# A one-core transformer kernel: the first stage's norm, columns and operand splits rearranged over the engines

## The chip, the cores and the metric

The kernel runs on one core of one Trainium2 chip. The metric is device time in microseconds (us), from the start of the program to its end; the time before is the median of three runs. In the profile, PE is TensorE's matmul, PEld its weight load, DVE is VectorE, ACT is ScalarE, POOL is GpSimd and SP is the SyncE queue, from which every load is issued.

## What is computed

The reference is two model blocks in a row on 512 positions of width 1024, all in float32. Only the start of the first block matters here:

```python
mod = cond @ ada_w[layer] + ada_b[layer]          # cond = silu(c)
sh1, sc1, g1, sh2, sc2, g2 = jnp.split(mod, 6, axis=-1)
h = _modulate(_rmsnorm(x, norm1_g[layer]), sh1, sc1)   # h*(1+scale)+shift
y = _pool_mixer(h, pool_w_in, pool_w_grp, pool_scale, pool_w_out)
x = x + g1 * y
h = _modulate(_rmsnorm(x, norm2_g[layer]), sh2, sc2)
x = x + g2 * _conv_ffn(h, ...)
```

Layer 0 uses the pooling mixer, layer 1 a dilated attention with keys and values of their own modulated norm; both have the gated FFN with a short convolution. The second block (retention, stick-breaking attention, FFN) follows.

## The kernel before

**Layout.** x is held as eight tiles x[m] of 128 channels by 512 positions. Weights come as 434 units of 512 KB (eight 128x128 tiles), in the order of their use.

**Exact products from three.** An operand t is split into a high part h (rounded on ACT) and a low part l = t - h; `mm3` (L243) multiplies high by high, high by low and low by high, so one float32 product is three matmuls (L244, L245, L246). A weight unit is split in `issue` (L176): ACT makes `wh` (L182), and `wl` (L184) is made by GpSimd for odd units while `st["spread"]` is set, else by VectorE. Activations are split by `split` (L310) and `modulate` (L479).

**The adaptive columns.** Each of 14 vectors (8 columns each) is a row-by-row dot product of a loaded 512 KB tile with `cond`, on VectorE. `ada_first` (L342) makes the scale and shift of the first norm from half tiles (L362, L364); `ada_chunk` (L329) makes the other 12, one column a step (L336), from tiles that share six `raw` buffers with the weight units.

**Order.** Tile schedules each engine's queue from a simulated list schedule, so the order on an engine need not be that of the text. PE's planner clock `pe["clk"]` adds 0.65 for a product; `pump` (L229) after each product lets side streams emit their next step once the clock is past their due time. Stream 2 is `ada_all` (L370): from clock 38.0, a step every `rate` (2.0 in the first stage, 6.0 afterwards). `need` (L379) forces missing steps at once.

**First stage**, `pool_mixer` (L526). Squares of x (ACT L400) are summed (`Stat`, L402), their mean taken by four one-column products on PE (L251), the root by Ln, Exp and four small VectorE instructions (L428 to L436), and spread to a 128x512 tile by four more products. x times that root is made by GpSimd for seven tiles (L544) and VectorE for one (L546). For each of eight input tiles: its columns (L362, L364, L566), `modulate` (VectorE L483, ACT L488, then the low part on VectorE or GpSimd, L489), then 24 matmuls into eight accumulators of PSUM (`us`). The second half of the last two tiles' products is put off to the end (`late`). Then come the evictions, the pooling bands (L593), the grouped product (`pool_w_grp`) and the output product (`pool_w_out`), whose results are added to x in `done` (L611, L612), which also feeds the next norm (L402) and splits x for it (L319).

**Norms further on.** A layer's next stage starts before its norm is known: `gemm_raw` (L288) multiplies raw x by the first four weight columns and corrects them later (`unraw`, L519: L521 and L522). Meanwhile `norm_gen` (L493), in stream 1, yields 2.5, takes the mean and root, yields 2.5, spreads it, multiplies all x (L473 or L475), and modulates. `conv_ffn` (L627) does so for both layers, `attention` (L900) for two modulated norms of one x (16 tiles).

Of the kernel before, what the change touches and what calls it, by code (L numbers as in the profile page):

```python
# [126 lines left out]
def model_kernel(ctx, tc, xT, wstream, adaw, vecs, crow, tab, rope, dret, selt, bandt, outT, plan, stop=None):  # L127
    nc = tc.nc
# [3 lines left out]
    sp = ctx.enter_context(tc.tile_pool(name="sp", bufs=60))  # L132
# [24 lines left out]
    for m in range(KT):  # L157
        nc.sync.dma_start(x[m], xT[m])
# [6 lines left out]
    nc.sync.dma_start(vec, vecs)  # L165
    nc.sync.dma_start(ct[:, :384], tab[:, :384])
# [7 lines left out]
    st = {"issued": 0, "used": 0, "spread": True}  # L174

    def issue():  # L176
        u = st["issued"]
        st["issued"] += 1
        raw = wp.tile([P, 8, P], F32, tag="raw", name=nm("raw"), bufs=6)
        nc.sync.dma_start(raw, wstream[u])  # L180
        h = wp.tile([P, 8, P], F32R, tag="wh", name=nm("wh"))
        nc.scalar.activation(h, raw, AF.Copy)  # L182
        l = wp.tile([P, 8, P], F32R, tag="wl", name=nm("wl"))
        (nc.gpsimd if u % 2 and st["spread"] else nc.vector).tensor_tensor(l, raw, h.bitcast(F32), op=ALU.subtract)  # L184
        units[u] = (h, l, raw)

    def wt(name, idx, k0, m0, n=1):
        i = st["used"]
        u, j = divmod(i, 8)
        if j == 0:  # L190
            while st["issued"] < min(u + 3, N_UNITS):
                issue()
            units.pop(u - 1, None)
# [135 lines left out]
    def ada_chunk(key):  # L329
# [12 lines left out]
    def ada_first(key):  # L342

        m = cp.tile([P, KT], F32, name=nm("mod"))
        mods[key] = m
        tiles = {}

        def load(j):
            for i in range(2):
                t = tiles[j, i] = S()  # L350
                nc.sync.dma_start(t, adaw[ADA_POS[key], j, :, i * T:i * T + T])

        load(0)
        yield
        for j in range(KT):
            col = small(2, "adaf")
            if j + 1 < KT:
                load(j + 1)
            for i in range(2):
                t = tiles.pop((j, i))  # L360
                half = slice(i * T, i * T + T)
                nc.vector.scalar_tensor_tensor(t, t, 1.0, cond[:, half], op0=ALU.mult, op1=ALU.mult,  # L362
                                               accum_out=col[:, i:i + 1])
            nc.vector.scalar_tensor_tensor(m[:, j:j + 1], col[:, 0:1], col[:, 1:2], ada_bias(key)[:, j:j + 1],  # L364
                                           op0=ALU.add, op1=ALU.add)
            yield
# [99 lines left out]

    def normed(R, residues):
        out = []
        for m in range(KT):
            t = S()  # L470
            if residues:
                to, r = (a.rearrange("p (r i) -> p r i", r=4) for a in (t, R))
                nc.vector.tensor_tensor(to, perm(x[m], 4), r, op=ALU.mult)  # L473
            else:
                nc.vector.tensor_tensor(t, x[m], R, op=ALU.mult)  # L475
            out.append(t)
        return out

    def modulate(xn, gs, sh, marks=None):  # L479
        hs = []  # L480
        for m in range(len(xn)):
            t = S()
            ts = nc.vector.tensor_scalar(t, xn[m], gs[:, m:m + 1], sh[:, m:m + 1], op0=ALU.mult, op1=ALU.add)  # L483
            if marks is not None:
                marks.append(ts.ins)
            h = S(F32R)
            l = S(F32R)
            nc.scalar.activation(h, t, AF.Copy)  # L488
            (nc.gpsimd if m % 2 else nc.vector).tensor_tensor(l, t, h.bitcast(F32), op=ALU.subtract)  # L489
            hs.append((h, l))  # L490
        return hs

    def norm_gen(stat, specs, out, residues):  # L493
        yield 2.5
# [3 lines left out]
        xn = normed(out["R"], residues)  # L498
        out["h"] = [modulate(xn, gs, sh) for gs, sh in specs]

    class RawNorm:


        def __init__(self, gs):
            self.stat, self.gs, self.raw = Stat(), gs, []
# [20 lines left out]
    def pool_mixer(g1, nx):  # L526

        stat = Stat(KT)
        for m in range(KT):
            stat.add(m)  # L530
        lnexp()
        scale_col, shift_col = ada_first((0, 1)), ada_first((0, 0))
        next(scale_col)
        next(shift_col)
        issue()
        next(scale_col)
        next(shift_col)
        Rp = spread(rstd(stat.mean()))
        R = S()
        nc.scalar.activation(R, Rp, AF.Copy)  # L540
        xn = [S() for _ in range(KT)]
        for m in range(KT):
            if m:
                nc.gpsimd.tensor_tensor(xn[m], x[m], R, op=ALU.mult)  # L544
            else:
                nc.vector.tensor_tensor(xn[m], x[m], Rp, op=ALU.mult)  # L546
# [4 lines left out]
        us = [[ps() for _ in range(NB)] for _ in range(2)]  # L551
        gs = cp.tile([P, KT], F32, name="gs0")
        h = []

        def half(i, kt, wH, wL):
            for b in range(NB):
                xH, xL = (a[:, b * P:(b + 1) * P] for a in h[kt])
                mm3(us[i][b], xH, xL, wH, wL, kt == 0, kt == KT - 1)

        late, marks = [], []  # L560
        for m in range(KT):
            if m:
                with tc.issue_after(marks[m - 1]):
                    next(scale_col)
                    next(shift_col)
            nc.vector.scalar_tensor_tensor(gs[:, m:m + 1], mods[(0, 1)][:, m:m + 1], 1.0, V("norm1_g", m),  # L566
                                           op0=ALU.add, op1=ALU.mult)
            h += modulate(xn[m:m + 1], gs[:, m:m + 1], mods[(0, 0)][:, m:m + 1], marks)
            for i in range(2):
                w = wt("pool_w_in", (0,), m * P, i * T, n=4)  # L570
                if i and m >= KT - 2:
                    late.append((m, w))
                else:
                    half(i, m, *w)
        for m, w in late:
            half(1, m, *w)
        ut = [[None] * NB for _ in range(2)]
        for i in range(2):
            for b in range(NB):
                t = ut[i][b] = S()  # L580
                if b % 2:
                    nc.scalar.activation(t, us[i][b], AF.Copy)
                else:
                    nc.vector.tensor_copy(t, us[i][b])
        nc.sync.dma_start(ct[:, 384:], tab[:, 384:])
        pooled = []
        for m in range(KT):
# [7 lines left out]
            pooled.append(split(o))  # L595
        ys = []
# [4 lines left out]
        g1 = g1()  # L601
        nx = nx()
# [14 lines left out]
        part(pss, ms, kts)  # L617
        for o, m in zip(pss, ms):
# [8 lines left out]
    def conv_ffn(l, nx, sh, gsh, g2, after):  # L627
# [3 lines left out]
        for half in range(2):  # L631
# [13 lines left out]
            it = gemms(outs, h)  # L645
# [531 lines left out]
    def next_norm(name, l, key):  # L1177
        def f():
            need(key)
            return RawNorm(gain(V(name, 8 * l, 8), mods[key]))  # L1180
        return f

    rate[0] = 2.0
    nx = pool_mixer(mod((0, 2)), next_norm("norm2_g", 0, (0, 4)))
# [208 lines left out]
```

## Time and profile before

| | us |
|---|---|
| median of 3 runs (lowest, highest) | 2739.53 (2738.41, 2740.74) |
| the profiled execution's own time | 2741.72 |
| its span, first to last instruction | 2740.0 |
| busy: PE / DVE / ACT / POOL | 2651.2 / 1435.7 / 993.5 / 391.4 |

The profile has one core, so the slowest core is the only one. A view of stretches gives the busy time of each engine between two times of the span, with the mean granted TensorE clock as a share of its full level. A view of waits lists for how long an engine sat idle and which instruction ended it. A timeline lists instructions in order, with the idle time just before one in brackets.

### The profile page before, as it was taken

The page shows a single profiled execution, that of the slowest core. Times are in us where ns is not written, and L with a number is a line of the kernel's source. Part 1 is how long each engine was busy: PE and PEld are TensorE (multiplying, and loading weights), DVE is VectorE, ACT ScalarE, POOL GpSimd, SP SyncE. Part 2 cuts the span into 40 slices and gives each one's busy share as a digit, 9 for nine tenths or more (in the row PEclk, how much of TensorE's full clock was granted, in tenths as well). Part 3 has the DMA queues.
Part 4 walks back from the last instruction along what each step waited for, and adds up shares of the span by engine and source line. Part 5 has one row for each costly group of instructions (what it writes and reads, how often), then busy time and mean ns, then how long its engine had stood idle before and what let it go on. Part 6 is the DMA issues. An engine that isn't in the chain of part 4 may idle for free. (4 is left out here: it accounts for less than half of the span.)

```text
span 2740.0 us, 32562 instructions
## 1 busy us (share of the span) xinstructions
PE 2651.2 (97%) x12952; PEld 2186.7 (80%) x12952; DVE 1435.7 (52%) x2146; ACT 993.5 (36%) x1673; POOL 391.4 (14%) x280
## 2 busy tenths in 40 slices
PE   6979999989999999999999999999999999999998
PEld 4868888868788887788888887888888887888887
DVE  8997566782434335853444347543344347543342
ACT  3334233344343443442344451422233451422223
POOL 3220000131212121300003111110111011110111
PEclk9989999999999999999999999999999999999999
DMA  8755555432222222232323211322323211232221
GB/s 293 254 182 189 176 173 173 140 126 75 70 78 73 74 70 78 75 99 97 100 92 116 85 64 52 100 94 98 100 93 118 89 63 54 93 100 94 99 99 47
DMA packets 86231, 297.69 MB, mean 109 GB/s; under 512 B 9574, under 2 KB 10302, under 8 KB 86078
## 3 DMA queue, kind: packets, MB, share of 16 engines
q1 hardware_dynamic: 86078, 295.61, 32.6%
q8 instruction: 101, 1.65, 0.2%
q14 instruction: 52, 0.43, 0.0%
HBM read 293.48 MB, written 2.10 MB: 108 GB/s over the span
## 5 line engine op out<-in xcount | busy, mean ns | idle before, releaser
L244 PE MATMUL ps<-s,wh 128*128 128x512 f32 x3152 | 1244.9, 395 | 0.8 <-DVE s L917 0.6
L245 PE MATMUL ps<-s,wh 128*128 128x512 f32 x3152 | 1235.4, 392 | 6.3 <-POOL s L489 5.6
L246 PE MATMUL ps<-s,wl 128*128 128x512 f32 x3152 | 1232.9, 391 | 3.5 <-DVE wl L184 3.5
L182 ACT ACTIVATE wh<-raw 128x1024 fp32r<-128x1024 f32 x434 | 459.6, 1059 | 1037.6 <-PE ps L245 738.3
L184 DVE TENSOR_TENSOR wl<-raw,wh 128x1024 fp32r<-128x1024 f32 x384 | 481.8, 1255 | 481.1 <-ACT wh L182 468.6
L244 PEld LDWEIGHTS ps<-s,wh 128*128 128x128 f32 x3152 | 594.8, 189 | 132.3 <-issue 8.0
L245 PEld LDWEIGHTS ps<-s,wh 128*128 128x128 f32 x3152 | 595.4, 189 | 128.3 <-POOL s L489 8.5
L246 PEld LDWEIGHTS ps<-s,wl 128*128 128x128 f32 x3152 | 594.5, 189 | 129.3 <-DVE wl L184 3.9
L184 POOL TENSOR_TENSOR wl<-raw,wh 128x1024 fp32r<-128x1024 f32 x50 | 125.4, 2508 | 467.7 <-ACT wh L182 447.9
L402 POOL TENSOR_TENSOR s<-s,s 128x512 f32<-128x512 f32 x45 | 71.6, 1596 | 780.4 <-ACT s L400 727.2
L251 PE MATMUL ps<-s,s 128*64 128x128 f32 (+7 forms) x1376 | 153.6, 305 | 16.2 <-POOL s L1116 12.3
L251 PEld LDWEIGHTS ps<-s,s 128*128 128x128 f32 (+2 forms) x1376 | 122.3, 172 | 53.7 <-issue 17.6
L1149 POOL TENSOR_TENSOR s<-s,s 128x512 f32<-128x512 f32 x44 | 76.2, 1732 | 536.8 <-ACT s L421 536.8
L336 DVE SCALAR_TENSOR_TENSOR araw<-araw,cond 128x1024 f32<-128x1024 f32 x96 | 130.8, 1367 | 36.5 <-DMA araw<-in_adaw 34.6
L1151 DVE TENSOR_TENSOR s<-s,ps 128x512 f32<-128x512 f32 x44 | 30.3, 688 | 140.3 <-PE ps L246 127.8
L421 ACT ACTIVATE s<-s 128x512 f32<-128x512 f32 x96 | 59.7, 625 | 110.1 <-DVE s L653 86.4
L780 ACT ACTIVATE s<-s,st 128x128 f32<-128x128 f32 (+1 forms) x192 | 79.6, 417 | 41.5 <-DVE st L776 27.0
L315 ACT ACTIVATE s<-s 128x512 fp32r<-128x512 f32 x104 | 65.6, 631 | 61.8 <-POOL s L895 41.3
L316 DVE TENSOR_TENSOR s<-s,s 128x512 fp32r<-128x512 f32 x104 | 72.8, 700 | 25.7 <-ACT s L315 25.7
L1146 DVE TENSOR_TENSOR s<-ps,s 128x512 f32<-128x512 f32 x44 | 30.4, 691 | 106.4 <-PE ps L246 106.4
L244 PE MATMUL ps<-wh,s 128*128 128x512 f32 x192 | 77.7, 405 | 7.9 <-ACT s L488 7.9
L246 PE MATMUL ps<-wh,s 128*128 128x512 f32 x192 | 75.9, 397 | 6.1 <-DVE s L489 6.1
(182 smaller groups left out, 2077.8 us busy)
## 6 DMA issues: line engine op xcount, KB each, us to landing
raw<-in_wstream SPq DMA_DIRECT2D x434, 512.0 KB, 3.3
araw<-in_adaw SPq DMA_DIRECT2D x96, 512.0 KB, 4.0
s<-in_adaw SPq DMA_DIRECT2D x32, 256.0 KB, 6.0
x<-in_xT SPq DMA_DIRECT2D x8, 256.0 KB, 5.7
s<-in_dret SPq DMA_DIRECT2D x8, 256.0 KB, 4.8
out<-s SPq DMA_DIRECT2D x8, 256.0 KB, 2.9
s<-in_rope SPq DMA_DIRECT2D x4, 256.0 KB, 5.8
cond<-in_crow SPq DMA_DIRECT2D x1, 512.0 KB, 4.2
```

Source lines behind the costliest of these rows:

```text
L182: nc.scalar.activation(h, raw, AF.Copy)
L184: (nc.gpsimd if u % 2 and st["spread"] else nc.vector).tensor_tensor(l, raw, h.bitcast(F32), op=ALU.subtract)
L244: nc.tensor.matmul(out, wH, xH, start=start, stop=False, **kw)
L245: nc.tensor.matmul(out, wH, xL, start=False, stop=False, **kw)
L246: nc.tensor.matmul(out, wL, xH, start=False, stop=stop, **kw)
L251: nc.tensor.matmul(out, lhsT, rhs, start=start, stop=stop, **kw)
L315: nc.scalar.activation(h, src, AF.Copy)
L316: nc.vector.tensor_tensor(l, src, h.bitcast(F32), op=ALU.subtract)
L336: nc.vector.scalar_tensor_tensor(raw, raw, 1.0, cond, op0=ALU.mult, op1=ALU.mult, accum_out=col[:, j:j + 1])
L402: eng.tensor_tensor(self.ss, self.ss, q, op=ALU.add)
L780: nc.scalar.activation(e[:, c0:c0 + w], e[:, c0:c0 + w], AF.Exp, bias=st4[:, b, hh:hh + 1], accum_out=st4[:, b, 4 + hh:5 + hh])
L1149: nc.gpsimd.tensor_tensor(s, s, R, op=ALU.mult)
```

## The change

Every x load moves behind the first columns' loads. All loads for the eight input tiles are issued at the start, interleaved; six of the first eight weight units fit the `raw` buffers. The root of the norm is computed before any modulation. `prepare(m)` makes one input tile, one tile ahead of PE; the low part of the next weight unit is its last VectorE instruction. Inside the first stage every VectorE and ScalarE instruction is pinned behind the one traced before it on its engine. GpSimd does nothing there: `spread` starts off (attention still sets it), and the sum of squares for the next norm is VectorE's (`last` = 8). Modulation is two ACT instructions (high part and full value, each with scale and bias) and one VectorE subtraction, here and in every later modulated norm. Later columns get two load buffers of their own, and each column's VectorE instruction is pinned; their rate is 2.6 in the first stage, and they pause for 35.0 after it.

```diff
+            return tc.keep_in_program_order(r) if order["on"] else r   # Kept: vector, scalar
-    sp = ctx.enter_context(tc.tile_pool(name="sp", bufs=60))
+    sp = ctx.enter_context(tc.tile_pool(name="sp", bufs=58))
-    st = {"issued": 0, "used": 0, "spread": True}
+    st = {"issued": 0, "used": 0, "spread": False, "ahead": 3}
...
-            raw = wp.tile([P, D], F32, tag="raw", name=nm("araw"), bufs=6)
+            raw = wp.tile([P, D], F32, tag="araw", name=nm("araw"), bufs=2)
-            nc.vector.scalar_tensor_tensor(raw, raw, 1.0, cond, op0=ALU.mult, op1=ALU.mult, accum_out=col[:, j:j + 1])
+            tc.keep_in_program_order(nc.vector.scalar_tensor_tensor(
+                raw, raw, 1.0, cond, op0=ALU.mult, op1=ALU.mult, accum_out=col[:, j:j + 1]))
...
+    def modulated(xn, gs, sh, m):
+        kw = {"scale": gs[:, m:m + 1], "bias": sh[:, m:m + 1]}
+        h, t = S(F32R), S()
+        nc.scalar.activation(h, xn, AF.Identity, **kw)
+        nc.scalar.activation(t, xn, AF.Identity, **kw)
+        return h, t
+    def low(t, h):
+        l = S(F32R)
+        nc.vector.tensor_tensor(l, t, h.bitcast(F32), op=ALU.subtract)
+        return l
...
     def norm_gen(stat, specs, out, residues):
-        yield 2.5
+        yield 2.5 if residues else 4.5
...
+        if not residues:
+            for m in range(KT):
+                out["h"][0].append(modulate(normed(out["R"], m), *specs[0], m))
+            return
...
-        nc.vector.tensor_scalar(t, t, col, None, op0=ALU.add)
+        nc.scalar.activation(t, t, AF.Identity, bias=col)
...
     def pool_mixer(g1, nx):
+        order["on"] = True
         stat = Stat(KT)
+        sc, sh = AdaFirst((0, 1)), AdaFirst((0, 0))
+        nc.sync.dma_start(vec, vecs)
+        nc.sync.dma_start(ident, tab[:, C_ID:C_ID + P])
+        for m in range(KT):
+            sc.load(m)
+            sh.load(m)
+            if m == 0:
+                for i in range(KT):
+                    nc.sync.dma_start(x[i], xT[i])
+            fetch()
+        lnexp()
...
+        def prepare(m):
+            xn = normed(R, m)
+            hm, t = modulated(xn, gs, sh.cols, m)
+            if m + 1 < KT:
+                wh = issue_high()
+            if m + 2 < KT:
+                columns(m + 2)
+            h.append((hm, low(t, hm)))
+            if m + 1 < KT:
+                issue_low(*wh)
+        columns(0)
         for m in range(KT):
             stat.add(m)
+        o = stat.mean()
+        scale_column(1)
+        y = rstd(o)
+        wh = issue_high()
+        sh.column(1)
+        R = bcast(y)
+        issue_low(*wh)
+        us = [[ps() for _ in range(NB)] for _ in range(2)]
+        prepare(0)
+        for m in range(KT):
+            if m + 1 < KT:
+                prepare(m + 1)
+            for i in range(2):
+                wH, wL = wt("pool_w_in", (0,), m * P, i * T, n=4)
+                for b in range(NB):
+                    xH, xL = (a[:, b * P:(b + 1) * P] for a in h[m])
+                    mm3(us[i][b], xH, xL, wH, wL, m == 0, m == KT - 1)
+        order["on"] = False
...
-        g1 = g1()
-        nx = nx()
...
         part(pss, ms, kts)
+        g1 = g1()
+        nx = nx()
...
-            it = gemms(outs, h)
+            it = gemms(outs, h, first=2 if pre else 0)
...
-    rate[0] = 2.0
-    nx = pool_mixer(mod((0, 2)), next_norm("norm2_g", 0, (0, 4)))
+    rate[0] = 2.6
+    nx = pool_mixer(mod((0, 2)), next_norm("norm2_g", 0, (0, 4), KT))
...
     rate[0] = 6.0
+    streams[2].ready = pe["clk"] + 35.0
```

The evictions of `us` swap engines (even tiles to ACT, odd to VectorE), a `pump` is added after each pooled tile, the rest of the constant table is loaded after the input product, and the cast of two constants for the second block (L1237) is pinned to its place in the text.

## Rows read from the trace of the kernel before

**Rows 1.** The page's busy time of each engine over the whole span.
```profile
PE 2651.2 (97%) x12952; PEld 2186.7 (80%) x12952; DVE 1435.7 (52%) x2146; ACT 993.5 (36%) x1673; POOL 391.4 (14%) x280
```

**Rows 2.** Waits of PE, 0 to 220 us: total us, times, longest us.
```profile
PE ps L251 <- DVE s L402: 22.3, 2, 13.0
PE ps L244 <- ACT s L488: 7.9, 3, 6.0
PE ps L246 <- DVE s L489: 6.1, 4, 4.9
PE ps L246 <- DVE wl L184: 3.5, 1, 3.5
```

**Rows 3.** Waits of PE, 540 to 600 us (attention's start).
```profile
PE ps L255 <- ACT s L691: 7.1, 1, 7.1
PE ps L245 <- POOL s L489: 4.5, 3, 2.7
```

**Rows 4.** Waits of PE, 1110 to 1160 us (layer 1's FFN starts).
```profile
PE ps L251 <- DVE s L402: 5.0, 1, 5.0
```

**Rows 5.** Stretches: length; PE, PEld, DVE, ACT, POOL busy; granted clock, DMA share, GB/s.
```profile
10.00:20.00 10.00, 3.94 (x16) 3.57 (x16) 7.22 (x18) 4.74 (x9) 0.81 (x1) 1.00 1.04 395
24.40:80.10 55.70, 47.66 (x192) 36.97 (x193) 53.65 (x110) 13.54 (x17) 17.22 (x9) 1.00 0.72 254
...
142.40:190.90 48.50, 33.81 (x131) 27.14 (x132) 45.79 (x68) 14.27 (x22) 9.65 (x5) 0.82 0.58 196
190.90:550.00 359.10, 359.04 (x1590) 296.94 (x1589) 242.03 (x327) 124.68 (x157) 15.62 (x11) 1.00 0.53 169
550.00:594.00 44.00, 30.82 (x123) 23.04 (x125) 41.41 (x51) 16.07 (x24) 21.53 (x11) 0.84 0.48 165
...
1115.00:1153.00 38.00, 31.91 (x135) 25.61 (x134) 31.73 (x46) 12.37 (x19) 8.35 (x6) 0.87 0.31 97
```

**Rows 6.** Timeline, 19 to 50 us (start us, us, instruction): VectorE beside GpSimd's product, and alone.
```profile
19.19 11.19 POOL L544 TENSOR_TENSOR s<-x,s 128x512 f32<-128x512 f32 x7 [18.67 <-ACT s L540]
...
25.32 1.75 DVE L362 SCALAR_TENSOR_TENSOR s<-s,cond 128x512 f32<-128x512 f32 x1
...
43.20 0.68 DVE L362 SCALAR_TENSOR_TENSOR s<-s,cond 128x512 f32<-128x512 f32 x1
...
45.32 1.22 DVE L184 TENSOR_TENSOR wl<-raw,wh 128x1024 fp32r<-128x1024 f32 x1
46.46 0.69 DVE L489 TENSOR_TENSOR s<-s,s 128x512 fp32r<-128x512 f32 x1
...
48.90 0.22 DVE L364 SCALAR_TENSOR_TENSOR mod<-adaf,vec 128x1 f32<-128x1 f32 x1
```

**Rows 7.** Line L483, 538 to 588 us: ns min/median/max.
```profile
L483 DVE TENSOR_SCALAR s<-s,gain,mod x16: 531/550/2634, 546.8 to 586.4; 128x512 f32<-128x512 f32 x16
```

**Rows 8.** VectorE's groups by form, 538 to 588 us: busy us, mean ns.
```profile
L483 DVE TENSOR_SCALAR s<-s,gain,mod 128x512 f32<-128x512 f32 x16 | 17.6, 1106 | 0.0
```

**Rows 9.** Timeline of the start (in brackets: idle before it).
```profile
6.81 4.69 ACT L400 ACTIVATE s<-x 128x512 f32<-128x512 f32 x7
...
16.40 2.08 PE L251 MATMUL ps<-ct,rsy 128*128 128x128 f32 x8 [1.52 <-DVE rsy L436]
...
30.99 0.80 PE L246 MATMUL ps<-wh,s 128*128 128x512 f32 x1 [4.91 <-DVE s L489]
```

**Rows 10.** Timeline of the first stage's end: VectorE's last addition, PE's next mean.
```profile
158.29 0.74 DVE L612 SCALAR_TENSOR_TENSOR x<-ps,mod,x 128x512 f32<-128x512 f32 x1
...
160.82 1.87 PE L251 MATMUL ps<-one,s 128*128 128x1 f32 x8 [9.30 <-DVE s L402]
```

**Rows 11.** ACT's groups by form, 190.9 to 550 us: busy us, mean ns.
```profile
L182 ACT ACTIVATE wh<-raw 128x1024 fp32r<-128x1024 f32 x65 | 68.8, 1058 | 137.8 <-PE ps L245 103.4 <-issue 16.7 <-DMA araw<-in_adaw 9.1
...
L651 ACT ACTIVATE s<-s,vec 128x512 f32<-128x512 f32 x2 | 1.6, 804 | 0.0
```

**Rows 12.** Tile araw, 60 to 140 us: time of its loads from issue to landing.
```profile
DMA to landing us min/median/max: 3.2/4.7/8.0
```

More of the change, by code (lines that the diff above doesn't have):

```diff
@@ L185, in issue @@
         units[u] = (h, l, raw)
+    def issue():
+        issue_low(*issue_high())
     def wt(name, idx, k0, m0, n=1):
@@ L190, in wt @@
         if j == 0:
-            while st["issued"] < min(u + 3, N_UNITS):
+            while st["issued"] < min(u + st["ahead"], N_UNITS):
                 issue()
@@ L465, in gain, with normed, modulate @@
         return o
[L467 to L491, printed above, removed]
+    def normed(R, m, residues=False):
+        t = S()
+        if residues:
+            to, r = (a.rearrange("p (r i) -> p r i", r=4) for a in (t, R))
+            nc.vector.tensor_tensor(to, perm(x[m], 4), r, op=ALU.mult)
+        else:
+            nc.vector.tensor_tensor(t, x[m], R, op=ALU.mult)
+        return t
+    def modulated(xn, gs, sh, m):
[8 more added lines that the diff above has]
+        return l
+    def modulate(xn, gs, sh, m):
+        h, t = modulated(xn, gs, sh, m)
+        return h, low(t, h)
     def norm_gen(stat, specs, out, residues):
-        yield 2.5
+        yield 2.5 if residues else 4.5
         y = rstd(stat.mean())
@@ L497, in norm_gen, with __init__ @@
         out["R"] = bcast(y, residues)
-        xn = normed(out["R"], residues)
-        out["h"] = [modulate(xn, gs, sh) for gs, sh in specs]
+        out["h"] = [[] for _ in specs]
+        if not residues:
+            for m in range(KT):
+                out["h"][0].append(modulate(normed(out["R"], m), *specs[0], m))
+            return
+        xn = [normed(out["R"], m, True) for m in range(KT)]
+        for hs, spec in zip(out["h"], specs):
+            for m in range(KT):
+                hs.append(modulate(xn[m], *spec, m))
     class RawNorm:
-        def __init__(self, gs):
-            self.stat, self.gs, self.raw = Stat(), gs, []
+        def __init__(self, gs, last):
+            self.stat, self.gs, self.raw = Stat(last), gs, []
         def add(self, m):
@@ new lines, in pool_mixer, with scale_column, columns @@
+        lnexp()
+        def scale_column(m):
+            nc.vector.scalar_tensor_tensor(gs[:, m:m + 1], sc.column(m), 1.0, V("norm1_g", m), op0=ALU.add, op1=ALU.mult)
+        def columns(m):
+            scale_column(m)
+            sh.column(m)
+        h = []
+        def prepare(m):
[8 more added lines that the diff above has]
+                issue_low(*wh)
@@ L547, in pool_mixer @@
+        st["ahead"] = 3
+        order["on"] = False
         bands = [S() for _ in range(3)]
@@ L550, in pool_mixer @@
             nc.sync.dma_start(b[:, :n], bandt[:, 3 * i * BAND:3 * i * BAND + n])
[L551 to L577, printed above, removed]
+        nc.sync.dma_start(ct[:, P:], tab[:, P:])
+        ut = [[S() for _ in range(NB)] for _ in range(2)]
         for i in range(2):
             for b in range(NB):
-                t = ut[i][b] = S()
                 if b % 2:
-                    nc.scalar.activation(t, us[i][b], AF.Copy)
+                    nc.vector.tensor_copy(ut[i][b], us[i][b])
                 else:
-                    nc.vector.tensor_copy(t, us[i][b])
-        nc.sync.dma_start(ct[:, 384:], tab[:, 384:])
+                    nc.scalar.activation(ut[i][b], us[i][b], AF.Copy)
         pooled = []
```

87 lines of the change are left out of this document (43 added, 44 removed).

## The prediction

> **What bounds the kernel now.** I began with the page: PE is busy 97% of the span, no other engine over 52% [rows 1]. So time can only come from places where PE waits or runs at the low clock. The waits of PE say where: the first 220 us hold four kinds, nearly all behind VectorE's or ScalarE's part of a norm or of a tile [rows 2]; two later places matter, attention's start [rows 3] and layer 1's FFN [rows 4]. The view of stretches then sizes each [rows 5]. The reader is to see there that between 24.4 and 190.9 us VectorE is nearly always busy while PE is not, and that from 190.9 to 550 PE has no idle time at all. That stretch also gives the pace of full-clock work: 359.10 us over 1590 matmuls, 0.226 us each.
>
> What each place loses beyond that pace:
> - Input product, 24.4 to 80.1: 192 matmuls x 0.226 = 43.4 of 55.7 us, so 12.3 lost.
> - First norm2, 142.4 to 190.9: 108 matmuls (96 of `gemm_raw`, three products of the next) are 24.4 us, the mean, the spread and the column sums about 2.8; 21.3 lost. It is 14.7 idle (48.5 - 33.8) and some 6.6 at the low clock (mean 0.82).
> - Attention's start, 550 to 594: 13.2 idle, and of the 7.0 us that a mean clock of 0.84 withholds some 5 fall on work: 18.
> - Layer 1's FFN, 1115 to 1153: 6.1 idle, some 3 at the low clock: 9.
>
> Why VectorE is late shows in the timeline [rows 6]. The same column product takes 0.68 us alone and 1.75 us while GpSimd multiplies x, whose seven products cost 1.6 us each; the modulation L483 has a median of 0.55 us [rows 7] but a mean of 1.11 [rows 8] at attention's start, where GpSimd runs half the subtractions. The work is not too much; it is stretched by what runs beside it.
>
> **The start.** The change puts the vectors, the identity and four column halves before x: 0.2 + 0.07 + 1.05 MB, at 395 GB/s [rows 5] 3.3 us. The last Square now ends at 11.5 us [rows 9], so at 14.8, and with one addition the mean starts near 15.4 instead of 13.0 [rows 2]. VectorE's variance is queued behind `scale_column(1)`, whose tile lands one weight unit and one column later (1.05 MB, 2.7 us); its two products and two small steps end near 18.4, 1.1 us after the mean (1.87 long [rows 10]). From mean to spread's end takes 5.5 us today (13.0 to 18.48 [rows 2, 9]); so it ends at 22.0. Then VectorE in order: copy of the spread 0.6, `wl` of unit 0 1.14, x times root 0.6: 24.4; ACT's high part 0.8 [rows 11] gives the first matmul at 25.2, against 24.4. The third matmul needs the low part, behind `columns(2)` on VectorE: 28.1, where PE now resumes at 30.99 [rows 9]. Loads behind it come at 1.57 MB a tile, 4.0 us, faster than they are used; the seventh and eighth weight unit hold SP until a `raw` buffer is free, which costs nothing, since the buffers free from 24 us and what is queued behind is used after 50.
>
> **The input product.** Per tile VectorE has, by starts one after the other (1.22 us long, next start 1.14 later [rows 6]): x times root 0.61, four column products 2.44, three one-column steps about 0.6 (0.22 long, each waiting for the one before), subtraction 0.61, `wl` 1.14: 5.4 us. PE has 24 x 0.226 = 5.4. They balance, with VectorE one tile ahead and relieved after the sixth tile. ACT has 0.8 + 0.8 + 1.06 [rows 11] = 2.7 a tile, hidden. So PE runs from 28.1: 190 x 0.226 = 42.9, plus 1.8 for a cold beginning: 72.8 instead of 80.1. **7.3 us gained.** The bound on the good side is the 8.0 idle and 4.3 cold of this stretch; on the bad side VectorE's sum at its full lengths, 5.8 a tile, leaves 4.5. Eight accumulators now finish together; the bands need only the first four, done 2.7 us before the end, so the evictions stay hidden by the second four's products.
>
> **Bands to output product.** PE is busy 62.3 us there and stays so. VectorE gains ten-odd `wl` but loses the blocking. It holds 24 columns x 1.2.
>
> **First norm2.** After the fourth output tile VectorE has four `done` (0.66 + 0.61 + 0.66 each, the first 0.74 long [rows 10]) at once, then each 5.4 us tile brings 1.93 of `done`, 1.14 of `wl` and two columns, 2.4: 5.5. The backlog of about 5 us stays to the end. The later yield (4.5, so seven products instead of four) covers 2 of it. I take 4 us of waiting at the mean instead of 9.3 [rows 10] and 3.5 before it [rows 2], 1 at the column sums, 1 at the low clock: 6 of 21.3 remain, **15.3 gained.** Bounds: 1 and 14 remaining. The first normal product takes two outputs at a time, so it uses a tile each 1.36 us where ACT makes one in 1.4 to 1.75 (two of 0.8 less overlap, plus its share of `wh`), with ten us of start; no wait there.
>
> **Attention's start.** L483 leaves VectorE (17.6 us [rows 8]), eight subtractions come from GpSimd (4.9), and the blocking by GpSimd shrinks to its `wl`. But columns pause for 35 us after the first stage and step each 6.5 (ten products): at `nx2` 51 of the 56 wanted exist, and five are forced onto VectorE just there, 6 us, pinned. VectorE is busy 41.4 of these 44 us [rows 5]; less 17.6, plus 4.9, plus some 3 net for forced columns and less blocking, it is 32. ACT does 32 activations; the values' evictions, for which PE's transposes wait 7.1 us now [rows 3], stand behind them, and PE reaches them 22 us after the raw product. I take 5 us remaining of 18: **13 gained** (bounds 3 and 18).
>
> One rule speaks against this part. The rows: unblocked, a scale-and-shift is one VectorE instruction of 0.55 us [rows 7]; the change makes it two of 0.80 on ACT [rows 11]. The Trainium skill, ScalarE: Activation LUTs, section Rules for kernel authors, puts adds and multiplies on VectorE and not on ScalarE; by it this part loses, and the total would be the second rival's 2714 instead of 2701. The trace bears the rule out for one instruction alone; but ACT is busy 36% of the span [rows 1], and VectorE is what PE waits for, so I count the part as a gain.
>
> **Layer 1's FFN.** The mean is put three products, 2 us, later, so 5.0 of waiting [rows 4] becomes 3, and GpSimd's subtractions go: **3 gained** (bounds 0 and 7). Elsewhere PE has no cover to lose; the moved cast is 0.3 us on VectorE, hidden behind products. The columns that slide into attention are 1.2 us of VectorE each 6.5 us, on an engine busy 52% over the span [rows 1]; between 0 and 2 us, I take 0.
>
> **Sum.** 7.3 + 15.3 + 13 + 3 = 38.6. The profiled execution took 2741.7 us, 1.7 more than its span and 2.2 more than the median of the runs; 2741.7 - 38.6 - 2.2 = 2701.
>
> **Rivals.**
> - *VectorE stays late.* Program order means that an instruction waiting for ACT or a load holds all behind it. For it: VectorE has no margin per tile in the input product, and 0.1 us too little in the second half of the output product. Then 4.5, 9 and 5 remain of the gains, and 1 elsewhere: 19.5, so 2720.
> - *ScalarE becomes the bound.* If each pair of activations runs without overlap with `wh` between, 16 tiles take 31 us, the value evictions land where PE wants them or after, and the 7.1 us wait [rows 3] mostly stays, 8 lost there, 5 at the two FFN norms: 2714. Against: ACT's low load. (The Trainium skill's rule above comes to this here.)
> - *Slower: the two column buffers.* A pinned column whose tile has not landed stops VectorE. A buffer's round is landing + 0.3 issue + 1.2 product, and two share it. At the median landing of 4.7 us [rows 12] a column can come each 3.1 us, at the pace of 2.7 asked for nearly enough. At the worst landing, 8.0, it is 4.75: 24 columns take 114 us instead of 65, VectorE reaches the mean 49 us late: 2750. It decides above a landing of 7.2 us. Against: the demand of 0.29 MB a us is below the 395 GB/s seen.
> - *Nothing comes of it:* PE's waits only move, 2738.
>
> **How the numbers follow.** Chances: the forecast 0.64 (its own range 2688 to 2714), VectorE late 0.17, ScalarE 0.08, slower 0.07, nothing 0.04. Faster by over 0.2% (5.5 us, about what a measurement of this kernel can tell) is 0.64 + 0.17 + 0.08 = 0.89; same 0.04; slower 0.07. The range 2686 to 2724 reaches over the first three cases: its low end is every bound on the good side but a few us, its high end the late VectorE with 4 more.
>
> **What would show it.** Right: no GpSimd work in the first 400 us but four small memsets; PE resumes near 28 us and the input product ends near 73; column products all near 0.68 us; the wait at the first norm2's mean 2 to 6 us; PE's L691 wait gone at attention's start; idle time of PE in all near 60 us instead of 88.8 [rows 1]. Wrong: a wait at the variance or the first spread beyond 24 us, gaps between tiles before 73, columns waiting for their loads (idle of VectorE put down to araw), or a L691 wait that is still there.

## The result and the profile after

| | before | changed |
|---|---|---|
| median of 4 runs each, us | 2738.97 | 2710.32 |
| lowest, highest | 2738.22, 2740.74 | 2709.82, 2713.44 |
| the profiled execution's own time | 2741.72 | 2713.44 |
| its span | 2740.0 | 2711.7 |

The ratio is 0.9897, with a 95% interval of 0.988 to 0.9914. The forecast was 2701 with a range of 2686 to 2724: the sign and the range held, and 28.7 us were gained instead of 38.6. The profiled execution is the slowest of its four, 3.1 above their median; the clock of the second block, below, can account for that.

In the changed kernel every VectorE and ScalarE instruction goes through one helper and shows line L140, so its groups are told apart by their tiles. `mm3` is L274 to L276, the one-column and spread products L281, the transposes L285. The page's busy times, beside [rows 1]:

```profile
PE 2645.2 (98%) x12952; PEld 2184.3 (81%) x12952; DVE 1399.8 (52%) x2137; ACT 1029.9 (38%) x1720; POOL 320.0 (12%) x242
```

PE's idle time went from 88.8 to 66.5 us (span less busy). The other 6.0 us are busy time, for the same 12952 matmuls; the granted clock over the span went from 0.990 to 0.993. PE's waits from 0 to 220 us, which answer to [rows 2]:

```profile
PE ps L281 <- DVE s L140: 18.4, 2, 16.1
PE ps L274 <- ACT s L140: 3.4, 1, 3.4
```

Two of the four kinds are gone: nothing waits for a low part of a tile (6.1) or of a weight unit (3.5). Of the 18.4, 16.1 is the start and 2.2 the mean of the first norm2, which was 9.3 [rows 10]. The stretches, which answer to [rows 5] (the input product, first norm2, on to the end of attention's raw product, attention's start, layer 1's FFN):

```profile
24.90:71.00 46.10, 46.04 (x194) 37.95 (x195) 41.23 (x96) 22.43 (x29) 0.00 (x0) 1.00 0.82 305
140.20:159.80 19.60, 17.36 (x90) 14.75 (x89) 16.53 (x28) 10.66 (x15) 0.00 (x0) 1.00 0.60 190
159.80:522.70 362.90, 361.58 (x1601) 298.72 (x1601) 243.68 (x325) 138.44 (x178) 14.95 (x9) 1.00 0.51 166
...
552.00:594.00 42.00, 35.85 (x239) 27.92 (x240) 33.26 (x62) 15.43 (x44) 4.43 (x2) 0.92 0.57 188
1089.00:1126.00 37.00, 32.49 (x141) 26.47 (x141) 26.52 (x40) 17.57 (x24) 1.79 (x2) 0.91 0.31 101
```

In the first two GpSimd is at zero and the clock at 1.00; the input product runs with no gap. In attention's start PE still stands 6 of 42 us, and the clock is at 0.92. Following the same points (the same matmul, counted from the start) through both traces gives the balance:

| point of PE's program | before | changed | gained so far |
|---|---|---|---|
| first matmul of the input product | 24.4 | 25.0 | -0.5 |
| input product ends | 80.3 | 70.9 | 9.3 |
| first normal product of the first FFN | 186.8 | 159.8 | 27.1 |
| attention's raw product ends | 549.95 | 522.66 | 27.3 |
| first transposes in attention | 589.1 | 552.0 | 37.1 |
| value products, second head group | 841.42 | 813.21 | 28.2 |
| layer 1's FFN, last product before its mean | 1117.20 | 1089.00 | 28.2 |
| second block begins | 1645.97 | 1615.34 | 30.6 |
| last matmul ends | 2731.80 | 2703.51 | 28.3 |

So the first stage and its norm gave nearly all of the gain. Attention's start first gained 10 more and gave 9 of them back within 130 us. What takes them is in the waits from 480 to 600 us (beside [rows 3]):

```profile
PE ps L285 <- ACT s L140: 7.0, 9, 2.1
PE ps L281 <- DVE s L140: 3.7, 2, 3.4
```

The one wait of 7.1 has become nine short ones of the same sum: 1.5 us where it stood, and eight in front of the softmax's transposes. VectorE's timeline there:

```profile
553.88 1.21 DVE L140 SCALAR_TENSOR_TENSOR araw<-araw,cond 128x1024 f32<-128x1024 f32 x1
...
559.65 0.55 DVE L140 SCALAR_TENSOR_TENSOR s<-ct,ps 128x384 f32<-128x384 f32 x1
560.86 1.23 DVE L140 SCALAR_TENSOR_TENSOR araw<-araw,cond 128x1024 f32<-128x1024 f32 x1 [0.66 <-DMA araw<-in_adaw]
...
562.01 0.28 DVE L140 TENSOR_REDUCE st<-s 128x1 f32<-128x128 f32 x1
562.21 0.16 DVE L140 TENSOR_TENSOR mod<-adac,vec 128x8 f32<-128x8 f32 x1
...
562.61 0.16 DVE L140 SCALAR_TENSOR_TENSOR gain<-mod,vec 128x8 f32<-128x8 f32 x1
```

Between a score's addition (ended at 560.20) and its maximum (562.01) a column product waits for its load and runs, 1.8 us in all. Twelve such columns stand between 553.9 and 587.3, after 29.8 us in which none ran (524.1 to 553.9). Four of them are forced by the request for the output norm's scale: the column at 560.86 is the 80th, which completes the vector (562.21) that this scale (562.61) is made of. The other eight belong to the next vector, which nobody asks for yet; they come closely behind. The expectations below call all twelve forced, which the trace corrects.

### The profile page after: what moved, and what is told of

Its sections match the earlier page's. It is cut to its first block, busy times and chain, and to the rows that moved or that the text cites. A ratio compares the mean times of both kernels' runs of the same rounds, so it can differ in the third digit from the quotient of the medians.

```text
span 2711.7 us, 32544 instructions
## 1 busy us (share of the span) xinstructions
PE 2645.2 (98%) x12952; PEld 2184.3 (81%) x12952; DVE 1399.8 (52%) x2137; ACT 1029.9 (38%) x1720; POOL 320.0 (12%) x242
## 4 chain that ended last, share of the span: by engine, by line
PE 61%; DVE 2%; POOL 1%; issue 0%; ACT 0%; DMA 0%; SPq 0%; DVEq 0%; POOLq 0%
PE ps L274 19%; PE ps L275 18%; PE ps L276 18%; PE ps L281 4%; DVE s L140 1%; PE ps L285 1%; POOL s L1165 0%; DVE x L140 0%; DVE wl L140 0%; ACT s L140 0%; PE ps L774 0%; PE ps L773 0%; PE ps L772 0%; PE ps L1071 0%; PE ps L1070 0%
## 5 line engine op out<-in xcount | busy, mean ns | idle before, releaser
L274 PE MATMUL ps<-s,wh 128*128 128x512 f32 x3152 | 1241.4, 395 | 0.2 <-DVE s L140 0.2
L276 PE MATMUL ps<-s,wl 128*128 128x512 f32 x3152 | 1230.8, 391 | 0.0
L140 ACT ACTIVATE wh<-raw 128x1024 fp32r<-128x1024 f32 x434 | 459.4, 1059 | 1024.1 <-PE ps L275 783.2
L140 DVE TENSOR_TENSOR wl<-raw,wh 128x1024 fp32r<-128x1024 f32 x394 | 492.2, 1249 | 494.5 <-ACT wh L140 482.7
L274 PEld LDWEIGHTS ps<-s,wh 128*128 128x128 f32 x3152 | 593.4, 188 | 129.6 <-issue 7.2
L276 PEld LDWEIGHTS ps<-s,wl 128*128 128x128 f32 x3152 | 593.2, 188 | 125.1 <-issue 1.1
L140 ACT ACTIVATE s<-s 128x512 fp32r<-128x512 f32 (+6 forms) x288 | 167.9, 584 | 182.0 <-DVE s L140 118.6
L140 DVE TENSOR_TENSOR s<-s,s 128x512 fp32r<-128x512 f32 (+3 forms) x202 | 140.4, 698 | 75.6 <-ACT s L140 74.9
L140 DVE TENSOR_TENSOR s<-ps,s 128x512 f32<-128x512 f32 (+6 forms) x164 | 103.8, 647 | 139.0 <-PE ps L276 128.8
L281 PE MATMUL ps<-s,s 128*64 128x128 f32 (+7 forms) x1376 | 156.9, 309 | 16.9 <-POOL s L1165 12.6
L140 DVE TENSOR_TENSOR s<-s,ps 128x512 f32<-128x512 f32 x108 | 73.1, 686 | 194.1 <-PE ps L276 168.2
L281 PEld LDWEIGHTS ps<-s,s 128*128 128x128 f32 (+2 forms) x1376 | 124.5, 174 | 55.3 <-issue 17.9
L211 POOL TENSOR_TENSOR wl<-raw,wh 128x1024 fp32r<-128x1024 f32 x40 | 99.8, 2494 | 414.4 <-ACT wh L140 368.5
L140 ACT ACTIVATE s<-ps 128x512 f32<-128x512 f32 (+5 forms) x188 | 97.0, 530 | 114.1 <-PE ps L281 66.9
L140 DVE COPY s<-ps 128x512 f32<-128x512 f32 (+2 forms) x73 | 48.7, 673 | 148.2 <-PE ps L285 77.1
L140 DVE SCALAR_TENSOR_TENSOR araw<-araw,cond 128x1024 f32<-128x1024 f32 x96 | 119.0, 1242 | 10.4 <-DMA araw<-in_adaw 10.4
L140 ACT ACTIVATE s<-s,st 128x128 f32<-128x128 f32 (+1 forms) x192 | 79.7, 417 | 52.3 <-DVE st L140 52.3
L140 ACT ACTIVATE s<-x 128x512 f32<-128x512 f32 x72 | 45.1, 626 | 95.2 <-DVE x L140 92.7
```

The source lines that it names most:

```text
L140: r = f(*a, **kw)
L274: nc.tensor.matmul(out, wH, xH, start=start, stop=False, **kw)
L276: nc.tensor.matmul(out, wL, xH, start=False, stop=stop, **kw)
L281: nc.tensor.matmul(out, lhsT, rhs, start=start, stop=stop, **kw)
```

## The experiments

**The forced columns: two ways to move them.** One makes the columns faster in layer 0's FFN, so that none has to be forced at attention's start; the other asks for them only after the loop over the heads.

```diff
-    rate[0] = 6.0
+    rate[0] = 5.0
```

> The columns' rate after the first stage is 5.0 instead of 6.0, so that all 56 columns exist when attention asks for them and none is forced there. Theory: the twelve column products that now stand among the first softmax steps make the transposes wait and cost the 8 to 9 us that are given back between 552 and 683 us, so 2701 to 2704. Rival: the first attention branch is limited by its own chain of scores, maxima, exponentials and turned blocks, and the columns only fill VectorE's holes: 2709 to 2712. A third possibility is that the columns, made more densely, hold up the layer 0 FFN: then that stretch grows by up to 3 us and eats a part of the gain.

```diff
             pre.append(t)
-        nx2 = nx2()
-        stat = nx2
...
                     streams[0].add(combine(parts, done))
+        nx2 = nx2()
+        stat = nx2
         out_proj(0, done, g1, stat)
```

> The call that asks for the scale of attention's output norm is moved behind the loop over the heads, so the same twelve columns are made one by one during attention, at rate 6, and not at its start. Theory of the forced columns: 2700 to 2704, with the first transposes at 552 us as before and the waits for their inputs gone. Rival of the branch's own chain: 2709 to 2712. If this one and the one with rate 5.0 agree within 2 us, the place of the columns is what matters and not how many are made in the FFN.

Measured: 2705.35 (ratio 0.9876, 0.9861 to 0.9891) and 2705.98 (0.9877, 0.9863 to 0.9892). Both are 4 to 5 us below the changed kernel; their intervals still overlap its own a little, so the traces decide. The waits from 500 to 700 us with the later request, and its stretch 552 to 594:

```profile
PE ps L281 <- DVE s L140: 7.0, 3, 3.3
PE ps L285 <- ACT s L140: 1.5, 1, 1.5
```
```profile
552.00:594.00 42.00, 40.23 (x301) 34.16 (x302) 30.46 (x59) 18.91 (x53) 4.76 (x2) 1.00 0.41 138
```

Eight of the nine transposes' waits are gone, PE is busy 40.2 instead of 35.9 us, and the clock is back at 1.00. From the end of attention's raw product to the value products of the second head group the kernels take 290.6 us (changed), 283.8 (rate 5.0) and 284.4 (later request), so the forcing and the crowd behind it cost 6.2 to 6.8 us. That is the theory's cause, at three quarters of its size. The number of columns is not what counts: with the later request seven still run between 552 and 594. Both runs also undo a second effect, which no run separates: `need` sets the planner's clock forward for each step that it forces, and with it the due times of the other streams. With the later request some comes back where the columns now run, as one wait of 2.6 us and a low clock near 675 us. With rate 5.0 the first transposes wait 4.9 us for VectorE instead, and more than that is gained behind them. There, too, the first norm2's mean waited 3.6 instead of 2.2 and a low clock followed (0.84 over 140 to 162); that is ahead of the edit, and no run here explains it.

**GpSimd in the first stage.** Two of its jobs were given back, one at a time.

```diff
-    st = {"issued": 0, "used": 0, "spread": False, "ahead": 3}
+    st = {"issued": 0, "used": 0, "spread": True, "ahead": 3}
```

> GpSimd makes the low part of every second weight unit in the first stage again, everything else as changed. Theory of blocking: VectorE's two-input instructions grow from 0.68 to between 1.2 and 1.75 us beside it, and since VectorE has no margin in the input product and in the second half of the output product, 4 to 12 us come back: 2714 to 2722. Rival: VectorE is relieved of 1.14 us in every second unit and that pays for the blocking: 2708 to 2712.

Measured 2720.08 (0.9931, 0.9914 to 0.9948): the theory of blocking by its time. (The flag also holds in layer 0's FFN, where nothing is lost: this run is 11.0 us behind at that FFN's first normal product and at attention's raw product alike.) PE's waits from 0 to 220 us have `wl` and a tile's low part in them again:

```profile
PE ps L276 <- DVE wl L140: 4.4, 2, 2.8
PE ps L281 <- DVE rsy L140: 3.8, 2, 2.2
...
PE ps L276 <- DVE s L140: 3.2, 2, 1.7
```

What is stretched differs from the theory. In the input product the column products keep their 0.68 us; three one-column steps take about 2.2 us instead of 0.22, each until the GpSimd instruction beside it ends. GpSimd's instruction, then the step:

```profile
38.68 2.54 POOL L211 TENSOR_TENSOR wl<-raw,wh 128x1024 fp32r<-128x1024 f32 x1 [9.30 <-DMA s<-in_adaw]
```
```profile
39.03 2.21 DVE L140 SCALAR_TENSOR_TENSOR mod<-adaf,vec 128x1 f32<-128x1 f32 x1
```

The kernel before has three such steps in its input product too (2.31, 2.37 and 2.43 us, at 30.86, 49.76 and 61.08).

```diff
-            xn = normed(R, m)
+            xn = S()
+            (nc.gpsimd if m else nc.vector).tensor_tensor(xn, x[m], R, op=ALU.mult)
```

> In the first stage GpSimd multiplies seven of the eight x tiles by the root again, everything else as changed. Theory of blocking: the column products beside those 1.6 us multiplications take up to 1.75 instead of 0.68 us, and as nothing holds GpSimd back it runs them one after the other from about 24 us, over the first three tiles of the input product, where VectorE has least in hand: 4 to 11 us are lost, 2714 to 2721, all of it before 75 us. Rival: VectorE is relieved of 0.61 us a tile and is a tile ahead: 2707 to 2712.

Measured 2714.50 (0.9912, 0.9898 to 0.9927), the low end of the theory; the trace is 6.6 us behind at the first norm2, all of it lost before 36 us. GpSimd's and VectorE's timelines of this run:

```profile
22.46 11.88 POOL L590 TENSOR_TENSOR s<-x,s 128x512 f32<-128x512 f32 x7 [21.95 <-DVE s L140]
```
```profile
25.11 1.75 DVE L140 SCALAR_TENSOR_TENSOR s<-s,cond 128x512 f32<-128x512 f32 x1
...
28.59 1.12 DVE L140 SCALAR_TENSOR_TENSOR mod<-adaf,vec 128x1 f32<-128x1 f32 x1
29.75 1.21 DVE L140 SCALAR_TENSOR_TENSOR gs<-mod,vec 128x1 f32<-128x1 f32 x1
30.88 0.68 DVE L140 SCALAR_TENSOR_TENSOR s<-s,cond 128x512 f32<-128x512 f32 x1
```

Three column products take 1.75 us beside GpSimd [rows 6], though not all (the one at 30.88 takes 0.68), and a one-column step of 0.22 [rows 6] takes 1.1. VectorE was relieved of seven products, and was later for it.

**The order by hand.** Once for the whole first stage, once only from the input product on.

```diff
     def pool_mixer(g1, nx):
-        order["on"] = True
+        order["on"] = False
```

> VectorE and ScalarE are no longer kept in program order in the first stage (the later columns stay pinned). Theory: the order by hand keeps the next weight unit's low part and the next tile's operands ahead of work that nobody waits for; without it the input product gets gaps again and 2 to 8 us are lost: 2712 to 2718. Rival: once GpSimd is out of it the simulated schedule's order is about the same, 2709 to 2712. The third possibility, that the order by hand makes VectorE wait where it could work, gives 2705 to 2708.

Measured 2742.70 (1.001, 1.0001 to 1.002), outside all three expectations: without the pinning the whole gain is gone. PE's waits from 0 to 220 us:

```profile
PE ps L281 <- DVE s L140: 50.5, 2, 48.2
PE ps L274 <- ACT s L140: 2.4, 1, 2.4
```

The mean starts at 48.2 instead of 16.1 us, since the additions of squares now run from 41.8 us on, behind most of the column products, whose loads VectorE waits for (15.0 us, six times, against 5.5, once). Little more is lost from there on: the first norm2's mean is 31.6 us late and the second block 33.7. The kernel before had no such pinning and its mean started at 13.0 [rows 2], which points to the new order of loads as what needs it; no run tests that.

```diff
         issue_low(*wh)
+        order["on"] = False
         us = [[ps() for _ in range(NB)] for _ in range(2)]
```

> The pinning ends when the root has been spread, so only the start is kept in program order. In the kernel without any pinning the first matmul came at 56.1 instead of 25.0 us, and the first norm2's mean 31.5 us late, so all of its loss lay ahead of the input product. Theory: the pinning is worth nothing from there on, 2708 to 2712. Rival: within the input product it keeps the next tile's operands ahead of the columns, and the unpinned start hid that because all columns had been made by then: 2713 to 2720, with gaps of TensorE between 30 and 72 us.

Measured 2712.39 (2707.38 to 2712.53; 0.9893, 0.9878 to 0.9907), not apart from the changed kernel; the input product ends at 70.9 in both, and the second block begins within 0.4 us of it. The pinning is worth 32 us in the start and nothing behind it.

This run also shows what the second block does by itself. Its code is the same in these two kernels, yet the granted clock differs. The stretches around the last two norms of the changed kernel, then of this run:

```profile
1665.00:1680.00 15.00, 12.18 (x50) 8.98 (x50) 5.89 (x19) 0.41 (x2) 1.26 (x1) 0.77 0.11 35
2286.00:2300.00 14.00, 11.19 (x46) 8.17 (x45) 5.46 (x15) 0.00 (x0) 1.26 (x1) 0.76 0.11 37
```
```profile
1662.00:1677.00 15.00, 12.18 (x63) 9.57 (x62) 8.57 (x22) 1.53 (x4) 2.55 (x2) 1.00 0.11 35
2280.00:2294.00 14.00, 11.19 (x58) 8.78 (x57) 8.17 (x18) 1.44 (x2) 2.55 (x2) 1.00 0.12 37
```

The waits before them are the same, the longest 2.8 us. A mean of 0.77 over 15 us withholds 3.4 us, and twice that is 6.8; the spans differ by 6.0 (2711.7 and 2705.7). The profile of the kernel before has half as much in these places (0.91 over 20 us and 0.89 over 15, 1.8 and 1.7 us), so the clock can also account for the 2.3 that the balance above loses after 1615 us.

**The order of TensorE.**

```diff
-        gpsimd, sync, tensor = tc.nc.gpsimd, tc.nc.sync, tc.nc.tensor
+        tensor = Kept(tc.nc.tensor)
+        gpsimd, sync = tc.nc.gpsimd, tc.nc.sync
```

> TensorE is kept in program order in the first stage too, so that the third matmul waits for the first low part as the prediction had it, and does not run the other accumulators' high-part products meanwhile. Theory: the 1.9 us by which the input product ended earlier than predicted, and more, come from that order: PE stands from 25.4 to between 28 and 30 us, the product ends at 73 to 76 us, 2712 to 2716. Rival: VectorE sets the pace of the tiles and the gap is made up later: 2709 to 2711.

Measured 2713.09 (2709.82 to 2714.04; 0.9903, 0.9888 to 0.9917): by the times not apart from the changed kernel. By the trace, 3.4 us later at the input product's end and 4.8 at the second block. PE's timeline of the changed kernel, then of this run:

```profile
24.96 0.80 PE L274 MATMUL ps<-wh,s 128*128 128x512 f32 x1 [3.36 <-ACT s L140]
25.55 0.63 PE L275 MATMUL ps<-wl,s 128*128 128x512 f32 x1
...
30.17 1.09 PE L276 MATMUL ps<-wh,s 128*128 128x512 f32 x4
```
```profile
25.15 0.80 PE L140 MATMUL ps<-wh,s 128*128 128x512 f32 x1 [3.36 <-ACT s L140]
25.74 0.63 PE L140 MATMUL ps<-wl,s 128*128 128x512 f32 x1
28.05 1.22 PE L140 MATMUL ps<-wh,s 128*128 128x512 f32 x2 [1.68 <-DVE s L140]
```

In the changed kernel the schedule takes the two high-part products of all eight accumulators first, and the first that needs a low part starts at 30.17, when it has long been made. In program order PE stands 1.7 us for it, and the gap is not made up.

**The modulation.**

```diff
     def modulate(xn, gs, sh, m):
-        h, t = modulated(xn, gs, sh, m)
-        return h, low(t, h)
+        t, h, l = S(), S(F32R), S(F32R)
+        nc.vector.tensor_scalar(t, xn, gs[:, m:m + 1], sh[:, m:m + 1], op0=ALU.mult, op1=ALU.add)
+        nc.scalar.activation(h, t, AF.Copy)
+        (nc.gpsimd if m % 2 else nc.vector).tensor_tensor(l, t, h.bitcast(F32), op=ALU.subtract)
+        return h, l
```

> In every modulated norm after the first, the modulation is made as before: scale and shift in one VectorE instruction, high part by ScalarE, odd low parts by GpSimd. Theory: this part is a gain, mostly at attention's start (predicted 13 us for all that changed there) and a little at the two FFN norms, so undoing it gives 2716 to 2724. Rival, the ScalarE rule (a scale and shift belongs on VectorE): it is a loss or nothing, 2704 to 2712.

The second run has `nc.vector` alone in the subtraction's line.

> As the run beside it, but the low parts stay on VectorE, so GpSimd stays out and only scale and shift move from two ScalarE instructions to one VectorE and one ScalarE instruction. If it was GpSimd's subtractions that made the old form slow, this one is near the changed kernel, 2708 to 2714, or better; if it was VectorE's load, it stands with the old form or above it, 2716 to 2726 (16 instructions of 0.55 us more at attention's start, 9 us, and 4 at each FFN norm).

Measured 2723.31 (0.9945, 0.993 to 0.996) and 2721.91 (0.9935, 0.9919 to 0.9952). It was VectorE's load; GpSimd's half of the subtractions isn't told apart from nothing (1.4 us between the two, whose intervals overlap). The second run's waits from 520 to 600 us:

```profile
PE ps L285 <- DVE s L140: 7.7, 1, 7.7
PE ps L281 <- DVE s L140: 7.7, 2, 5.6
PE ps L285 <- ACT s L140: 2.6, 3, 2.2
```

The first transposes wait 7.7 us for VectorE instead of 1.5 for ScalarE. From the raw product's end to the second head group's values it takes 299.3 us, 8.7 more than the changed kernel; another 4.9 is lost ahead of that, from a mean that waits 3.2 and a low clock behind it (0.84 over 140 to 162 us). The run with rate 5.0, whose modulation is the changed kernel's, has the same loss in the same place (4.7), so only the 8.7 are shown to be the modulation's.

**The first norm2's mean.**

```diff
-        yield 2.5 if residues else 4.5
+        yield 2.5
...
-    nx = pool_mixer(mod((0, 2)), next_norm("norm2_g", 0, (0, 4), KT))
+    nx = pool_mixer(mod((0, 2)), next_norm("norm2_g", 0, (0, 4)))
```

> The norm after the first stage gets back its shorter yield (2.5 instead of 4.5, for layer 1's FFN too) and GpSimd's six additions of squares. Theory: the yield covers 2 of the wait that is left at the mean, and GpSimd's additions of some 1.6 us stretch VectorE's work of the last four output tiles; the mean waits 5 to 8 us instead of 2.2, with some of the low clock that followed before, and layer 1's FFN loses its 0.5: 2714 to 2720. Rival: the wait went because the backlog of columns and low parts went, so both are without weight: 2709 to 2712.

Measured 2719.99 (0.9925, 0.9908 to 0.9941). The mean waits 7.6 us, and from 142.7 us on the clock is at its lower level; the stretch:

```profile
142.00:153.00 11.00, 7.85 (x23) 6.52 (x24) 8.95 (x18) 3.33 (x6) 0.00 (x0) 0.53 0.62 191
```

So the yield and the additions on VectorE are worth 9.7 us together, 9.2 of them by the first normal product of the FFN. The wait can be divided by the trace: the mean stands 13 matmuls earlier in PE's order than in the changed kernel (some 2.9 us at 0.226), and its input comes 2.6 us later. The low clock behind it belongs to both, so the shares of the 9.7 weren't told apart.

Three parts of the first stage were undone one at a time: the low parts, the products of x and this one. They put the first normal product 11.0, 6.8 and 9.2 us later, 27.0 in sum, beside the 27.1 that the balance gives to that point. No run undoes them together, so that they add up is not shown.

**One column buffer,** to try the slower rival's price.

```diff
-            raw = wp.tile([P, D], F32, tag="araw", name=nm("araw"), bufs=2)
+            raw = wp.tile([P, D], F32, tag="araw", name=nm("araw"), bufs=1)
```

> The later columns get one load buffer instead of two. By the third rival's sum a round is the landing, 4.2 us between 60 and 200 us, 0.3 of issue and 1.2 of product, so a column can come each 5.7 us where 2.7 is asked for: the 24 columns of the first stage take 137 us instead of 65, TensorE waits for them at the first norm2, and the twelve forced at attention's start take 68 us: 2760 to 2810. If instead columns have slack that two buffers hide, 2710 to 2730.

Measured 2745.68 (1.0023, 1.0014 to 1.0032). Tile araw in the changed kernel from 60 to 152 us, then in this run from 60 to 200:

```profile
L140 DVE SCALAR_TENSOR_TENSOR araw<-araw,cond x24: 1209/1216/1227, 63.6 to 138.8; 128x1024 f32<-128x1024 f32 x24
...
DMA to landing us min/median/max: 3.1/3.6/5.0
```
```profile
L140 DVE SCALAR_TENSOR_TENSOR araw<-araw,cond x24: 1215/1226/1228, 63.6 to 182.6; 128x1024 f32<-128x1024 f32 x24
...
DMA to landing us min/median/max: 3.1/3.4/4.3
```

A column each 5.2 us (119 / 23), for a round of 3.4 + 0.3 + 1.2 = 4.9: the price per column was right. What it costs was overestimated, and the time lies between the two expectations: PE waited 9.1 and 24.1 us where 72 had been expected, since products go on while columns are late, and attention's start lost nothing more. With two buffers a column comes each 3.3 us.

**Towards the best version.** The later request, and a later mean in both FFN norms.

```diff
-        yield 2.5 if residues else 4.5
+        yield 2.5 if residues else 8.0
```

> The later request for the output norm's scale, and the mean of both FFN norms put off by 8.0 instead of 4.5, five products of 0.68 us more. Theory: the mean waits 0 instead of 2.2 in the first norm2 and about 1.3 instead of 4.5 at layer 1's, with less low clock, and the tiles are still ready when the raw product ends 6 us after the spread: 2699 to 2703. Rival: the wait moves on to the spread or the first normal product: 2704 to 2708.

Measured 2700.82 (2698.92 to 2703.41; 0.9856, 0.9841 to 0.987), below the changed kernel's interval and inside the theory's range. Its waits from 1060 to 1160 us:

```profile
PE ps L281 <- DVE rsy L140: 3.5, 1, 3.5
PE ps L281 <- DVE s L140: 0.5, 1, 0.5
```

The mean's wait went (0.5 and 0.0), but moved on to the spread, 3.5 us at layer 1's FFN and 1.2 at the first norm2, as the rival said. By the trace it is 1.6 us ahead of the later request alone at the second block; the rest of the 5 us between the two medians isn't shown, and their intervals overlap.

## Why the prediction was right in sign and 10 us too low

- **The start** came as forecast: spread's end 21.6 (22.0), first matmul 25.0 (25.2).
- **Input product**, 7.3 forecast, 9.3 measured. The step that failed is "the third matmul needs the low part, behind `columns(2)` on VectorE: 28.1". The low part does come then: TensorE in program order resumes at 28.05. But with eight accumulators open the schedule has 16 high-part products to run first. The 1.8 us for a cold beginning have no row behind them. The runs show 2.2: the first ten matmuls start 0.43 us apart (24.96 to 29.39), later ones 0.23. The granted clock reads 1.00 there, but the trace's first record of it is at 29.6 us, so no row shows the cause.
- **First norm2**, 15.3 forecast, 17.8 measured up to its first normal product. I left 6 us (mean 4, column sums 1, clock 1); what is left is the mean's 2.2, at a clock of 1.00. The 2 us given to the later yield were too little: undoing it together with the additions on VectorE puts that product 9.2 us later. (The 108 matmuls of the working are 105, 96 and three products of three; the slip is 0.7 us.)
- **Attention's start**, 13 forecast, 0.9 measured (291.5 to 290.6 us from the raw product's end to the second head group's values). This is where the time is missing. The step that failed is "I take 5 us remaining of 18", drawn from VectorE's sum: the sum came out (32 of 44 us forecast, 33 of 42 measured), and so did the columns that exist at `nx2` (51 forecast, 52 measured, so four forced instead of five). But a VectorE with room in its sum doesn't keep PE from waiting: twelve columns crowd in between score and maximum, in the chain that PE waits for through ScalarE, and moving them gives back 6.2 to 6.8 us. The modulation's gain was there, 8.7 us. Both prices are taken from the changed kernel, one at a time; no run changes both.
- **The ScalarE rule.** VectorE's one scale-and-shift against ScalarE's two was 11.6 us slower in this kernel (2721.91 against 2710.32), 8.7 of it at attention's start. The Trainium skill, ScalarE: Activation LUTs, section Rules for kernel authors, would have it on VectorE. The trace agrees for one instruction alone (0.55 against 0.80 us); for the kernel's time the measurement decides against it, since here PE's first transposes waited 7.7 us for VectorE in the one form and 1.5 for ScalarE in the other. That the part is a gain was right.
- **Layer 1's FFN**, 3 forecast, 2.4 measured up to the second block, in part by luck. The step "the mean is put three products, 2 us, later" failed: in PE's order the mean comes only two matmuls later than before, and its wait went from 5.0 to 4.5. PE's two waits there for GpSimd's subtractions, 1.1 us together, are gone as forecast. With the yield of 8.0 it comes 18 matmuls later still, and the wait is 0.5. From the mean to the second block, the run with GpSimd's subtractions loses 1.0 us against the changed kernel and the one with the shorter yield 0.7.
- **Second block**, nothing forecast, -2.3 in the profile: within what the clock does from one execution to another, as above. With 0.2 us between the places, 9.3 + 17.8 + 0.2 + 0.9 + 2.4 - 2.3 make the 28.3 by which the last matmul ends earlier.
- The rivals: VectorE stays late holds in small at attention's start, where a maximum stands behind a pinned column that waits 0.66 us for its load. The two column buffers decide nothing at a landing of 3.6 us: a column comes each 3.3 us, near the 3.1 of the forecast.

## What to carry to other kernels

Work that is forced at one point is priced by what it stands between, not by the engine's busy share: look at which chain is running when it comes, and ask for it later if its result is needed later. Count in the trace what was really forced. An engine that is busy half the time can still be the one that everything waits for; taking even slower instructions off it pays if the engine that gets them isn't in that chain. Where program order is pinned, find out which stretch needs it: here one start was worth all of it. And a step put later in the text is later on the engine only if the schedule lets it be: check its place in the engine's order.

## What was unexpected of the hardware

- Beside GpSimd the smallest VectorE instructions were stretched the most. A step on a single column took 2.2 us instead of 0.22 beside a GpSimd instruction of 2.54, and 1.1 to 1.2 beside a run of GpSimd's products of 1.7 each. So what it paid was GpSimd's length and not its own.
- The second block, which no edit touches, took 1082.4 to 1088.2 us in the profiles of the changed kernel and its variants. After the same waits, the longest 2.8 us, the granted clock was 0.77 over the next stretch in one execution and 1.00 in another, 3.4 us each time. A difference of that size in a profile need not come from an edit elsewhere.
